# Two attentions with column-half value products, full-height score passes and single column sums: a change to block 2 of a two-block transformer kernel

## The chip, the core and the metric

The kernel runs on one core of one Trainium2 chip. The metric is the device time of one execution in microseconds (us), as a median of several runs. The core's engines are named as in the profile: PE multiplies matrices, PEld is the loading of its stationary operand, DVE, ACT and POOL are the vector, scalar and GpSimd engines, SP issues the transfers. A product on PE takes a stationary operand (rows of contraction by output rows) and streams a moving operand through it, column by column; the result lands in one of eight PSUM banks of 128 partitions by 512 fp32 columns. A row of the profile that says `128*64 128x512` is a stationary operand of 128 rows by 64 columns with 512 moving columns.

## What is computed

Two transformer blocks run over 512 tokens of width 1024, all in float32 precision. Only block 2's mixer matters in detail:

```python
u = rms_norm_2(h, mix_norm[i]);  proj = u @ w_in[i]
c_q, c_kv, k_rope, sb_qkv, gates = jnp.split(proj, SPLITS, axis=-1)
...
o_mla = causal_softmax_attention(q, k, v_mla)          # 8 heads, 96 wide, values 64 wide
o_sb = stick_breaking_attention(sq, sk, sv)            # 8 heads, 64 wide, values 64 wide
g_mla, g_sb = jnp.split(jax.nn.sigmoid(gates), 2, axis=-1)
merged = g_mla * (o_mla @ w_branch_mla[i]) + g_sb * (o_sb @ w_branch_sb[i])
h = h + merged @ w_out[i]
```

The stick-breaking weights are `exp(log_sigmoid(z) + suffix)`, where `suffix` sums `log_sigmoid(-z)` over the keys behind; they need no division. The softmax weights of the latent heads do. Each block also has feed-forward parts, and every norm divides by the root of a mean of squares over the 1024 features.

## The kernel before

Activations are kept feature-major (features on the 128 partitions, the 512 tokens along the free axis). A product in float32 is made of three passes over exact parts: high by high, low by high and high by low (`lin`, lines 259 to 261), or is one float32 matmul that PE runs as two passes. Weights stream in from HBM; ACT and DVE split each piece (lines 247 and 248).

`mixer2` (from line 880) is block 2's attention part. It is written as generators, one for each head and one for each chunk of a projection, and the string `STEPS2` says in which order their steps are issued: a digit is a step of stick-breaking head `sb(h)`, a letter a step of latent head `mla(h)`, `.` and `,` a step of the large projections, which fill PE's time while ACT and DVE work on a head. A scheduler then settles each engine's order from that.

A stick-breaking head has three steps. The first makes the scores `z` (lines 942 to 944): for each of four key blocks a pass of the stacked keys (high and low halves on 128 rows) against the queries, a bf16 pass that adds the mask (stationary operand: an identity), and a pass of the 64 rows of high keys against the queries' low part `ql`. The second makes the suffix sums. The third is the value product (line 984): the head's weights `za` stream past a 64-column piece of the values, and the result takes one half of a PSUM bank, the partitions 0 to 63 for even heads, 64 to 127 for odd ones. Two heads share the bank, and when both are in, ACT and DVE split it into exact parts (`split`, lines 310 and 311).

A latent head has five steps: transposes of queries and keys (line 1113), scores and softmax (lines 1128 to 1137; ACT adds up each row's sum), transposes of the weights (`et`, line 1144), the value product (line 1155), and, for each second head, four transposes (line 1169) and a split. In the value product the weights are stationary and 64 columns of values stream, token-major: 10 blocks of 128 by 128, two passes each. DVE then multiplies each token block by the reciprocal of its sum (line 1160). PSUM is shared out as two banks for projections, three for scores, two ("t") for transposes and one ("o") for the value products.

A norm's sum of squares (`Squares`) is kept as two tiles: ACT squares the chunks of features, POOL adds the first seven into `acc`, the last stays in its own tile. `colsum` (line 335) sums both over the partitions on PE with a moving operand of one column of ones: for each of four token blocks one matmul of `acc` and one of the last square, in two passes each.

## Time and profile before

| | us |
|---|---|
| median of 3 runs | 2273.33 (2273.32 to 2273.71) |
| span of the profiled execution | 2267.5 |
| own time of the profiled execution | not given; the runs lie 5.8 above the span |
| PE busy | 2247.1 (99%) |
| PEld, DVE, ACT, POOL busy | 1870.9, 1151.6, 881.5, 119.6 |

Busy times are shares of the span, not proof of a bound: a busy PE may be streaming, loading or draining. The stage that the change touches most lies between 1420 and 1840 us of the span. Most readings below go by when one instruction on PE starts and when the next does, since the printed length of a pass includes its overlap with the next.

### The profile page before, as it was taken

Reading aid. Unit: us, or ns where it says so; the run is one execution under the profiler, and the core shown is the slowest. Engines: PE = TensorE matmul, PEld = TensorE weight load, DVE = VectorE, ACT = ScalarE, POOL = GpSimd, SP = SyncE. Lnnn points to the kernel's source line nnn. Section 1 sums busy time; section 2 is a strip of 40 time slices with the busy share of each in tenths; the row PEclk is TensorE's granted clock in tenths of the full one; section 3 lists DMA queues with packets and bytes.
Section 4 is the critical chain, followed back from the end, with each engine's and each line's share of the span. In section 5 each row is a group of like instructions: output and inputs, shape, how many; then the busy total and the mean of one; then the engine's idle time right before and its main releaser. Section 6 shows DMA issues by size and latency. Waiting matters only on the chain.

```text
span 2267.5 us, 27653 instructions
## 1 busy us (share of the span) xinstructions
PE 2247.1 (99%) x11074; PEld 1870.9 (83%) x11074; DVE 1151.6 (51%) x1938; ACT 881.5 (39%) x1344; POOL 119.6 (5%) x156
## 2 busy tenths in 40 slices
PE   8999999999999999999999999999999999999999
PEld 7888888888788888889888888877778888888887
DVE  5644323778648444325644433476674654444334
ACT  4323223556635333223432322566654442233222
POOL 3000001000112000001000001000000010000000
PEclk9999999999889999999999999999999999999999
DMA  5333333322112333332333333321131233333331
GB/s 151 93 96 100 95 94 91 88 62 75 38 47 85 102 93 102 93 96 73 112 93 101 89 96 104 85 66 48 46 89 34 79 112 94 102 93 96 96 107 65
DMA packets 364836, 197.22 MB, mean 87 GB/s; under 512 B 10007, under 2 KB 356516, under 8 KB 364708
## 3 DMA queue, kind: packets, MB, share of 16 engines
q1 hardware_dynamic: 364100, 195.37, 30.0%
q8 instruction: 87, 1.43, 0.3%
q0 software_dynamic: 608, 0.09, 0.0%
q14 instruction: 41, 0.34, 0.0%
HBM read 193.33 MB, written 2.10 MB: 86 GB/s over the span
## 4 chain that ended last, share of the span: by engine, by line
PE 98%; DVE 1%; ACT 0%; DMA 0%; issue 0%; SPq 0%; DVEq 0%
PE f1o_p L260 2%; PE f2o_p L259 2%; PE f2o_p L260 2%; PE f1o_p L259 2%; PE f2o_p L261 2%; PE f1o_p L261 2%; PE f4o_p L259 2%; PE f3o_p L261 2%; PE f4o_p L261 2%; PE f3o_p L259 2%; PE f3o_p L260 2%; PE f4o_p L260 2%; PE gt_p L260 1%; PE gt_p L259 1%; PE gt_p L261 1%; PE f_p L260 1%
## 5 line engine op out<-in xcount | busy, mean ns | idle before, releaser
L248 DVE TENSOR_TENSOR f1o_l<-f1o_r,f1o_h 128x1024 fp32r<-128x1024 f32 (+1 forms) x24 | 27.3, 1136 | 76.6 <-ACT f1o_h L247 76.6
L248 DVE TENSOR_TENSOR f2o_l<-f2o_r,f2o_h 128x1024 fp32r<-128x1024 f32 (+1 forms) x24 | 27.3, 1136 | 76.6 <-ACT f2o_h L247 76.6
L247 ACT ACTIVATE f2o_h<-f2o_r 128x1024 fp32r<-128x1024 f32 (+1 forms) x24 | 23.8, 990 | 85.7 <-PE f2o_p L260 73.0
L247 ACT ACTIVATE f1o_h<-f1o_r 128x1024 fp32r<-128x1024 f32 (+1 forms) x24 | 23.8, 990 | 85.7 <-PE f1o_p L260 68.4
L247 ACT ACTIVATE f3o_h<-f3o_r 128x1024 fp32r<-128x1024 f32 (+1 forms) x24 | 23.8, 990 | 85.3 <-PE f3o_p L260 53.2
L247 ACT ACTIVATE f4o_h<-f4o_r 128x1024 fp32r<-128x1024 f32 (+1 forms) x24 | 23.8, 990 | 85.0 <-PE f4o_p L260 52.8
L376 POOL TENSOR_TENSOR f_acc<-f_acc,f_sq 128x256 f32<-128x256 f32 (+1 forms) x42 | 38.9, 927 | 316.9 <-ACT f_sq L375 299.5
L248 DVE TENSOR_TENSOR f3o_l<-f3o_r,f3o_h 128x1024 fp32r<-128x1024 f32 (+1 forms) x24 | 27.3, 1136 | 54.0 <-ACT f3o_h L247 54.0
L248 DVE TENSOR_TENSOR f4o_l<-f4o_r,f4o_h 128x1024 fp32r<-128x1024 f32 (+1 forms) x24 | 27.3, 1135 | 52.5 <-ACT f4o_h L247 52.5
L84 ACT ACT_TABLE_LOAD x36 | 46.2, 1283 | 1.4 <-PEq L1341 0.8
L376 POOL TENSOR_TENSOR m_acc<-m_acc,m_sq 128x256 f32<-128x256 f32 (+1 forms) x18 | 20.1, 1115 | 348.8 <-ACT m_sq L375 348.8
L260 PE MATMUL m1o_p<-mix_l,m1o_h 128*128 128x256 f32 (+1 forms) x88 | 29.3, 334 | 0.0
L261 PE MATMUL m1o_p<-mix_h,m1o_l 128*128 128x256 f32 (+1 forms) x88 | 29.2, 334 | 0.0
L259 PE MATMUL m1o_p<-mix_h,m1o_h 128*128 128x256 f32 (+1 forms) x88 | 28.6, 336 | 0.0
L376 POOL TENSOR_TENSOR pl_acc<-pl_acc,pl_sq 128x512 f32<-128x512 f32 x6 | 10.3, 1710 | 341.6 <-ACT pl_sq L375 341.6
L248 DVE TENSOR_TENSOR gt_l<-gt_r,gt_h 128x1024 fp32r<-128x1024 f32 x16 | 19.6, 1224 | 12.9 <-ACT gt_h L247 12.6
L94 ACT ACTIVATE l<-l 128x384 f32<-128x384 f32 (+1 forms) x48 | 24.2, 554 | 3.1 <-DVE l L949 3.0
L247 ACT ACTIVATE pg_h<-pg_r 128x1024 fp32r<-128x1024 f32 x8 | 8.5, 1061 | 42.6 <-PE pp L496 19.4
L94 ACT ACTIVATE e<-ms,mx,sck 128x512 f32<-128x512 f32 (+3 forms) x32 | 19.5, 614 | 14.0 <-DVE mx L1135 13.8
L260 PE MATMUL wo_p<-mg_l,wo_h 128*128 128x512 f32 x64 | 24.8, 390 | 0.0
L259 PE MATMUL wo_p<-mg_h,wo_h 128*128 128x512 f32 x64 | 24.8, 389 | 0.0
L376 POOL TENSOR_TENSOR f2p_acc<-f2p_acc,f2p_sq 128x512 f32<-128x512 f32 x6 | 7.7, 1288 | 322.9 <-ACT f2p_sq L375 322.9
(4287 smaller groups left out, 7533.5 us busy)
## 6 DMA issues: line engine op xcount, KB each, us to landing
f1o_r<-in_ffn_w_out_dram SPq DMA_DIRECT2D x16, 512.0 KB, 3.8
f2o_r<-in_ffn_w_out_dram SPq DMA_DIRECT2D x16, 512.0 KB, 4.3
f3o_r<-in_ffn_w_out_dram SPq DMA_DIRECT2D x16, 512.0 KB, 4.3
gt_r<-in_w_in_dram SPq DMA_DIRECT2D x16, 512.0 KB, 4.0
f4o_r<-in_ffn_w_out_dram SPq DMA_DIRECT2D x16, 512.0 KB, 4.1
f_r<-in_ffn_w_in_dram SPq DMA_DIRECT2D x12, 512.0 KB, 5.0
mg_r<-in_w_mix_in_dram SPq DMA_DIRECT2D x8, 512.0 KB, 4.0
m1o_r<-in_w_mix_out_dram SPq DMA_DIRECT2D x8, 512.0 KB, 4.2
```

What stands on the lines that cost most here:

```text
L84: ld = S.preload_act_table_set(name).ins
L94: i = S.activation(out, in_, func, **kw).ins
L247: S.activation(hi, raw, AF.Copy)
L248: V.tensor_tensor(lo, raw, hi.bitcast(F32), ALU.subtract)
L259: M.matmul(o, w[0], u[0], start=first, stop=False)
L260: M.matmul(o, w[0], u[1], start=False, stop=False)
L261: issued["last"] = M.matmul(o, w[1], u[0], start=False, stop=last).ins.name
L376: G.tensor_tensor(acc[:, sl], acc[:, sl], q[:, sl], ALU.add)
```

## The change

**Scores.** The low part of the queries is held in two tiles of 128 rows, one for each head, with zeros in the half that is not the head's own. POOL writes the zeros (eight of them, 64 by 512). The third pass of each piece is then 128 rows high, uses the same stationary keys as the first, and comes before the mask's pass.

**Value products.** `av_pair` issues the products of two heads in turn, key block by key block, one head into the lower and one into the upper half of one bank. It is called once both heads' weights are there, so the stick-breaking heads use four visits of PE, not eight. The latent heads now use the same form: the values are stationary (64 columns) and the transposed weights stream. The `et` transposes are as many as before, grouped by key block.

**Normalisation of the latent heads.** The result is feature-major at once, so the four transposes of the output go. The reciprocals of two heads (one DVE instruction) are widened by POOL to 128 by 512 (`rcw`), transposed by four PE instructions (`rcs`), copied to SBUF by ACT, and one DVE multiplication of 128 by 512 takes the place of eight of 128 by 64; the split reads that product from SBUF.

**Column sums.** In seven norms (three in block 1, three in block 2, one in the last part) one DVE addition of 128 by 512 joins the two tiles of squares, and `colsum` gets one tile.

**Order.** `STEPS2` is written anew for four steps a latent head. The order of the transfers on SP does not change.

The core of the diff (comments and docstrings that went are left out):

```diff
-STEPS2 = ('00..110,.3,2,2..3.4,,4.56241.56,,7,..s3567q.7ka.ba,cbca,,,d,a.,ccbdebg,,bdc.e..,.e.,.a.f,d,hgffd'
-          ',,e,gh,,eh,,f,,.,g,gh,fh')
+STEPS2 = ('00..110,.3,2,2..3.4,,4.56241.56,,7,..s3567q.7kaab,,bc,a,cd,b,de,ca,ef,db,fg,ec,gh,fd,h,ge,hfg'
+          '')
@@ Normed.factor (and the same two lines in ple)
-            r = token_rs(self.sq.parts, D, self.name)
+            acc, q = self.sq.parts
+            V.tensor_tensor(acc, acc, q, ALU.add)
+            r = token_rs([acc], D, self.name)
@@ sb_qk
-                ql = A(f"sql{j}", F32R)
-                for t, own in ((s0, lo), (s1, up)):
+                ql = [A(f"sql{j}{i}", F32R) for i in range(2)]
+                for t, l, own, other in ((s0, ql[0], lo, up), (s1, ql[1], up, lo)):
+                    G.memset(l[other, :].bitcast(F32), 0.0)
...
-                    V.tensor_tensor(ql[own, :], a[own, :], t[own, :].bitcast(F32), ALU.subtract)
+                    V.tensor_tensor(l[own, :], a[own, :], t[own, :].bitcast(F32), ALU.subtract)
@@ sb
                 M.matmul(z, k[:, b], q[:, t0:], start=True, stop=False)
-                M.matmul(z[:, d:d + P], identb, nst, start=False, stop=False)
-                M.matmul(z, k[own, b], ql[own, t0:], start=False, stop=True)
+                M.matmul(z, k[:, b], ql[:, t0:], start=False, stop=False)
+                M.matmul(z[:, d:d + P], identb, nst, start=False, stop=True)
...
-            other = pair.pop(h ^ 1, None)
-            o = pair[h] = px(f"osb{h}") if other is None else other
-            for c, l in enumerate(parts(za)):
-                M.matmul(o[own, c * P:], sv[c][:, h * 64:(h + 1) * 64], l, start=c == 0, stop=c == NT - 1)
-            if other is not None:
+            pair[h] = parts(za)
+            if h ^ 1 in pair:
+                o = px(f"osb{h}")
+                av_pair(o, lambda c, g: sv[c][:, g * 64:(g + 1) * 64], pair, h & ~1)
                 osb[h // 2] = split(o, f"osb{h}")
             yield
+        def av_pair(o, v, ps_, g):
+            for c in range(NT):
+                for i in (g, g + 1):
+                    M.matmul(o[64 * (i - g):64 * (i - g) + 64, c * P:], v(c, i), ps_[i][c], start=c == 0,
+                             stop=c == NT - 1)
@@ mla
-            ets = {}
-            for i, ts in enumerate(((3,), (2, 0), (1,))):
+            ets = [None] * NT
+            for i, ss in enumerate(((0,), (1, 3), (2,))):
                 ot, et = px(f"et{h}{i}", "t"), A(f"eT{h}{i}")
                 c = 0
-                for t in ts:
-                    for s in range(t + 1):
+                for s in ss:
+                    ets[s] = et[:, c:c + T - s * P]
+                    for t in range(s, NT):
                         M.transpose(ot[:, c:c + P], es[t][1][:, s * P:(s + 1) * P], ident)
-                        ets[t, s] = et[:, c:c + P]
                         c += P
...
-            oo = px(f"omla{h}", "o")
-            for t in (3, 2, 0, 1):
-                for s in range(t + 1):
-                    M.matmul(oo[:, t * 64:(t + 1) * 64], ets[t, s], vt[s][:, h * 64:(h + 1) * 64],
-                             start=s == 0, stop=s == t)
-            rc = tiny.tile([P, NT], F32, tag="rc", name=f"rc{h}")
-            V.reciprocal(rc, sums)
-            for t in range(NT):
-                V.tensor_scalar(om[t][:, h * 64:(h + 1) * 64], oo[:, t * 64:(t + 1) * 64], rc[:, t:t + 1], None,
-                                ALU.mult)
-            yield
-            j = h // 2
-            if omla[j] is None:
-                omla[j] = ()
-            else:
-                o = px(f"omT{j}", "t")
+            mpair[h] = ets
+            if h ^ 1 in mpair:
+                j = h // 2
+                oo = px(f"omla{j}", "o")
+                av_pair(oo, lambda c, g: vt[c][:, g * 64:(g + 1) * 64], mpair, h & ~1)
+                rc = tiny.tile([P, NT, 2], F32, tag="rc", name=f"rc{h}")
+                V.reciprocal(rc, msum[j])
+                sp, rw = px(f"rcs{j}", "t"), A(f"rcw{j}")
+                G.tensor_copy(rw.rearrange("p (t h n) -> p (t h) n", h=2, n=64),
+                              rc.rearrange("p t (h o) -> p (t h) o", o=1).to_broadcast([P, 2 * NT, 64]))
                 for t in range(NT):
-                    M.transpose(o[:, t * P:(t + 1) * P], om[t][:, j * P:(j + 1) * P], ident)
-                omla[j] = split(o, f"omT{j}")
+                    M.transpose(sp[:, t * P:(t + 1) * P], rw[:, t * P:(t + 1) * P], ident)
+                rs = A(f"rcs{j}")
+                S.activation(rs, sp, AF.Copy)
+                V.tensor_tensor(rs, oo, rs, ALU.mult)
+                omla[j] = split(rs, f"omT{j}")
```

How the order of instructions moves is shown at three places of PE. In the rows, what stands left of the arrow is written, right of it come the moving and then the stationary operand (for transposes the identity first); the trailing numbers are buffers.

**The scores of stick-breaking head 0**, the first two of its four pieces (`z` are banks, `sqk` queries and keys, `sql` the low part, `nst` and `identb` the mask's operands). Before:

```order
L942 MATMUL z00_11152<-sqk00_10962,sqk40_11004 128x512
L943 LDWEIGHTS identb_95
L943 MATMUL z00_11152<-nst_97,identb_95 128x128
L944 MATMUL z00_11152<-sql0_10965,sqk40_11004 128x512
L942 MATMUL z20_11154<-sqk00_10962,sqk40_11004 128x256
L943 LDWEIGHTS identb_95
L943 MATMUL z20_11154<-nst_97,identb_95 128x128
L944 MATMUL z20_11154<-sql0_10965,sqk40_11004 128x256
```

After:

```order
L944 MATMUL z00_11140<-sqk00_10947,sqk40_10992 128x512
L945 MATMUL z00_11140<-sql00_10950,sqk40_10992 128x512
L946 LDWEIGHTS identb_95
L946 MATMUL z00_11140<-nst_97,identb_95 128x128
L944 MATMUL z20_11142<-sqk00_10947,sqk40_10992 128x256
L945 MATMUL z20_11142<-sql00_10950,sqk40_10992 128x256
L946 LDWEIGHTS identb_95
L946 MATMUL z20_11142<-nst_97,identb_95 128x128
```

The pass of the low part has moved ahead of the mask's, next to the pass with the same keys, and reads a tile of its head's own; the later two pieces and the other heads follow suit.

**The stick-breaking value products.** Before, heads 2 and 4, both in the lower half of their banks (`za` followed by block and head, `sv` the values):

```order
L984 MATMUL osb2_12060<-za02_11551,sv0_11135 64x512
L984 MATMUL osb2_12060<-za12_11552,sv1_11137 64x384
L984 MATMUL osb2_12060<-za22_11553,sv2_11139 64x256
L984 MATMUL osb2_12060<-za22_11553,sv3_11141 64x128
L984 MATMUL osb4_12065<-za04_11822,sv0_11135 64x512
L984 MATMUL osb4_12065<-za14_11823,sv1_11137 64x384
L984 MATMUL osb4_12065<-za24_11824,sv2_11139 64x256
L984 MATMUL osb4_12065<-za24_11824,sv3_11141 64x128
```

After, heads 2 and 3, the first in the lower, the second in the upper half of one bank:

```order
L994 MATMUL osb3_12436<-za02_11540,sv0_11123 64x512
L994 MATMUL osb3_12436<-za03_11471,sv0_11123 64x512
L994 MATMUL osb3_12436<-za12_11541,sv1_11125 64x384
L994 MATMUL osb3_12436<-za13_11472,sv1_11125 64x384
L994 MATMUL osb3_12436<-za22_11542,sv2_11127 64x256
L994 MATMUL osb3_12436<-za23_11473,sv2_11127 64x256
L994 MATMUL osb3_12436<-za22_11542,sv3_11129 64x128
L994 MATMUL osb3_12436<-za23_11473,sv3_11129 64x128
```

Head by head has become head beside head. Three of the four stick-breaking pairs stand like this; the pair of heads 4 and 5 is cut in two visits of four rows. Of the latent pairs the first is spread over four visits (1, 1, 3 and 3 rows) and the other three stand whole.

**The end of the latent heads**, where the branch products `br` begin. Before (`omT` is the transposed output of a pair of latent heads, `om` the output of a token block):

```order
L1169 MATMUL omT2_14128<-ident_79,om3_13065 128x128
L261 MATMUL br03_p_14247<-omT0_h_13667,br03_0_l_14244 128x512
L259 MATMUL br03_p_14247<-omT1_h_13868,br03_0_h_14243 128x512
L260 MATMUL br03_p_14247<-omT1_l_13869,br03_0_h_14243 128x512
L261 MATMUL br03_p_14247<-omT1_h_13868,br03_0_l_14244 128x512
L1169 MATMUL omT3_14137<-ident_79,om0_13062 128x128
L1169 MATMUL omT3_14137<-ident_79,om1_13063 128x128
L1169 MATMUL omT3_14137<-ident_79,om2_13064 128x128
L1169 MATMUL omT3_14137<-ident_79,om3_13065 128x128
L259 MATMUL br00_p_14172<-omT2_h_14133,br00_0_h_14168 128x512
L259 MATMUL br01_p_14197<-omT2_h_14133,br01_0_h_14193 128x512
L259 MATMUL br02_p_14222<-omT2_h_14133,br02_0_h_14218 128x512
```

After (`rcs` are the transposed reciprocals, `eT` the weights, `vt` the values), with the end of pair 2's transposes and pair 3's value product:

```order
L261 MATMUL br03_p_14164<-omT1_h_13842,br03_0_l_14161 128x512
L1171 MATMUL rcs2_14024<-ident_79,rcw2_14025 128x128 x4
L994 MATMUL omla3_14038<-eT60_13943,vt0_12867 64x512
L994 MATMUL omla3_14038<-eT70_13995,vt0_12867 64x512
L994 MATMUL omla3_14038<-eT61_13950,vt1_12874 64x384
L994 MATMUL omla3_14038<-eT71_14002,vt1_12874 64x384
L994 MATMUL omla3_14038<-eT62_13957,vt2_12908 64x256
L994 MATMUL omla3_14038<-eT72_14009,vt2_12908 64x256
L994 MATMUL omla3_14038<-eT61_13950,vt3_12915 64x128
L994 MATMUL omla3_14038<-eT71_14002,vt3_12915 64x128
L259 MATMUL br00_p_14089<-omT2_h_14034,br00_0_h_14085 128x512
L259 MATMUL br01_p_14114<-omT2_h_14034,br01_0_h_14110 128x512
```

and a little later, the end of pair 3:

```order
L261 MATMUL br02_p_14139<-omT2_h_14034,br02_0_l_14136 128x512
L260 MATMUL br03_p_14164<-omT2_l_14035,br03_0_h_14160 128x512
L261 MATMUL br03_p_14164<-omT2_h_14034,br03_0_l_14161 128x512
L1171 MATMUL rcs3_14049<-ident_79,rcw3_14050 128x128 x4
L259 MATMUL br00_p_14089<-omT3_h_14059,br00_0_h_14085 128x512
L259 MATMUL br01_p_14114<-omT3_h_14059,br01_0_h_14110 128x512
```

Before, products of other tiles stood between the transposes and the first product that needs their result. Now `omla3`, which needs the one "o" bank, stands right behind `rcs2`, and the first product of `omT3_h` right behind `rcs3`. For pairs 0 and 1 eight transposes (of `qkT` and of `et`) stand between `rcs` and the next pair's value product.

## Rows read from the trace of the kernel before

**Rows 1.** The page, part 4: the chain that ended last, by engine.
```profile
PE 98%; DVE 1%; ACT 0%; DMA 0%; issue 0%; SPq 0%; DVEq 0%
```

**Rows 2.** Busy time by stretch of mixer2; stretch, length, busy times, PEclk, DMA, GB/s.
```profile
1460.00:1540.00 80.00, 80.00 (x354) 62.05 (x353) 59.41 (x97) 54.90 (x99) 0.00 (x0) 1.00 0.26 66
...
1620.00:1660.00 40.00, 40.00 (x201) 32.27 (x201) 33.93 (x138) 24.43 (x55) 0.00 (x0) 1.00 0.24 66
...
1420.00:1840.00 420.00, 420.00 (x2050) 333.43 (x2048) 260.29 (x571) 230.31 (x429) 11.66 (x7) 1.00 0.26 69
```

**Rows 3.** Timeline of PE, one head's scores; start, length (us), then the instruction.
```profile
1560.47 0.40 PE L260 MATMUL cq_p<-m_u6l,cq_h 128*128 128x512 f32 x1
1560.71 0.40 PE L942 MATMUL z<-sqk,sqk 128*128 128x512 f32 x1
1560.95 0.23 PE L943 MATMUL z<-nst,identb 128*128 128x128 bf16 x1
1561.11 0.50 PE L944 MATMUL z<-sql,sqk 64*128 64x512 f32 x1
1561.54 0.39 PE L942 MATMUL z<-sqk,sqk 128*128 128x256 f32 x1
...
1563.75 0.50 PE L261 MATMUL cq_p<-m_u6h,cq_l 128*128 128x512 f32 x1
```

**Rows 4.** Timeline of PE, a mask's pass of a latent head and its successor.
```profile
1699.53 0.22 PE L1129 MATMUL ms<-nts,identb 128*128 128x128 bf16 x1
1699.59 0.86 PE L1128 MATMUL ms<-qkT,qkT 96*128 96x384 f32 x2
```

**Rows 5.** Timeline of PE, value products: one head; two heads in the same half.
```profile
1542.74 0.39 PE L261 MATMUL gt_p<-m_u7h,gt_l 128*128 128x512 f32 x1
1543.06 2.37 PE L984 MATMUL osb<-za,sv 128*64 128x512 f32 x8
1545.36 0.50 PE L259 MATMUL cq_p<-m_u0h,cq_h 128*128 128x512 f32 x1
...
1565.78 4.52 PE L984 MATMUL osb<-za,sv 128*64 128x512 f32 x16
1570.23 0.50 PE L260 MATMUL gt_p<-m_u1l,gt_h 128*128 128x512 f32 x1
```

**Rows 6.** Timeline of PE, head 5's last two passes (upper half), head 6's eight (lower).
```profile
1608.96 2.38 PE L984 MATMUL osb<-za,sv 128*64 128x128 f32 x10
1611.27 0.38 PE L335 MATMUL cq_ss<-ones,cq_last 128*128 128x1 f32 x2
```

**Rows 7.** Timeline of PE, block 1: 512 columns in one, two and four column groups.
```profile
441.68 0.68 PE L663 MATMUL pd<-X 128*64 128x64 f32 x8
442.95 0.45 PE L663 MATMUL pd<-X 128*32 128x32 f32 x16
449.00 0.39 PE L663 MATMUL pd<-X 128*16 128x16 f32 x32
```

**Rows 8.** Timeline of PE, the last latent head's value product and what follows.
```profile
1775.88 2.34 PE L1155 MATMUL omla<-vt,eT 128*128 128x64 f32 x20
1778.05 0.61 PE L1169 MATMUL omT<-ident,om 128*128 128x128 f32 x4
1778.42 0.49 PE L261 MATMUL br_p<-omT_h,br_l 128*128 128x512 f32 x1
```

**Rows 9.** Timeline of PE, sixteen passes of a norm's column sum, first, last, successor.
```profile
2218.79 0.28 PE L335 MATMUL pl_ss<-ones,pl_acc 128*128 128x1 f32 x2
...
2220.27 0.36 PE L335 MATMUL pl_ss<-ones,pl_last 128*128 128x1 f32 x2
2220.50 0.48 PE L495 MATMUL pg<-pg_h,pl_u6h 128*128 128x512 f32 x1
```

**Rows 10.** Timelines of ACT and DVE behind the transposes of rows 8.
```profile
1778.70 0.60 ACT L310 ACTIVATE omT_h<-omT 128x512 fp32r<-128x512 f32 x1 [4.09 <-PE omT L1169]
...
1779.33 0.69 DVE L311 TENSOR_TENSOR omT_l<-omT,omT_h 128x512 fp32r<-128x512 f32 x1 [0.21 <-ACT omT_h L310]
```

**Rows 11.** Groups of POOL and of DVE: line, operation, count; busy, mean ns; idle.
```profile
L783 POOL COPY ws<-wd 128x128 f32<-128x128 f32 x4 | 1.2, 290 | 147.7 <-DVE wd L779 147.7
...
L1247 DVE TENSOR_TENSOR gate<-gate,gate 128x512 f32<-128x512 f32 x8 | 5.5, 688 | 0.0
```

**Rows 12.** Busy time of two stretches of block 1 with a stall; columns as in rows 2.
```profile
385.00:395.00 10.00, 8.82 (x61) 8.55 (x60) 9.90 (x25) 6.51 (x16) 3.09 (x5) 0.83 0.43 119
...
687.00:691.00 4.00, 2.93 (x23) 2.81 (x24) 3.85 (x9) 3.68 (x9) 0.59 (x1) 1.00 0.58 170
```

More of the change, by code (lines that the diff above doesn't have):

```diff
@@ L883, in mixer2 @@
         us, R, r = nx.factor()
-        sqk, sv, osb, pair, gate = {}, [], [None] * 4, {}, {}
+        sqk, sv, osb, pair, mpair, gate = {}, [], [None] * 4, {}, {}, {}
         bc = lambda a, n: a.rearrange("p (t o) -> p t o", o=1).to_broadcast([P, NT, n])
@@ L929, in sb @@
         def sb(h):
-            own = slice(64 * (h % 2), 64 * (h % 2) + 64)
-            q, k, ql = sqk[h // 2][h % 2], sqk[4 + h // 2][h % 2], sqk[h // 2][2]
+            q, k, ql = sqk[h // 2][h % 2], sqk[4 + h // 2][h % 2], sqk[h // 2][2][h % 2]
             width = (4 * P, 3 * P, 3 * P)
@@ L1076, in mixer2 @@
         sc, tk = (tiny.tile([P, NT, 8], F32, tag=f"sck{i}", name=f"sck{i}", bufs=1) for i in range(2))
-        qT, kT, om, omla = {}, {}, [], [None] * 4
+        qT, kT, msum, omla = {}, {}, {}, [None] * 4
         def head_factor(i, tl):
@@ L1117, in mla @@
             yield
-            if not om:
-                om.extend(A(f"om{t}") for t in range(NT))
-            sums = tiny.tile([P, NT], F32, tag="sums", name=f"sums{h}")
+            if h % 2 == 0:
+                msum[h // 2] = tiny.tile([P, NT, 2], F32, tag="sums", name=f"sums{h}")
+            sums = msum[h // 2][:, :, h % 2]
             es = [None] * NT
@@ L1287, in ple @@
                     pT.append(split(o, f"pT{j}"))
-                rs.append(token_rs(nx.sq.parts, D, "pl", behind=issued["last"]))
+                acc, q = nx.sq.parts
+                V.tensor_tensor(acc, acc, q, ALU.add)
+                rs.append(token_rs([acc], D, "pl", behind=issued["last"]))
                 table("sigmoid_and_others")
```

## The prediction

> **What bounds the kernel now.** I read the chain of waits first: PE has 98% of it [rows 1]. Then the busy time by stretch, for the stage that the change touches: between 1420 and 1840 us PE is busy in 420.00 of 420.00 us at a granted clock of 1.00 (2.4 GHz), DVE in 260.29, ACT in 230.31 and POOL in 11.66 [rows 2]. DVE comes nearest in the stretch from 1620, 33.93 of 40 us. So whatever PE no longer issues in this stage comes off the end, as long as nothing makes PE wait; and every new wait of PE is paid in full. How much a piece of PE work costs is not its printed length but the distance from its start to the start of what follows, so all prices below are differences of starts in the timeline of PE.
>
> **Scores.** One head's twelve passes run from 1560.71 to 1563.75 [rows 3]: 3.04 us. In them a 128-row pass of 512 columns takes 0.24 (1560.71 to 1560.95), the mask's pass 0.16, and the 64-row pass of 512 columns 0.43 (1561.11 to 1561.54): it is slow, and the mask ahead of it too, while a latent head's mask, followed by a pass of 96 rows, takes 0.06 [rows 4]. After the change a head has two 128-row passes for 1408 columns, 2816 in all at 0.24 for 512: 1.32 us. The masks lie between 4 x 0.06 and 4 x 0.16; no row shows a mask between two full-height passes, so I take 0.11, 0.44 in all. That is 1.76 a head, 1.28 saved, times eight **10.2 us** (8.6 with the dear mask, 11.8 with the cheap one). The zeros for the low part cost eight instructions on POOL, which is idle there [rows 2], and are written before the subtraction that fills the other half; I price them at nothing. Were they late, the first score pass of a pair would wait about as long as a POOL instruction of that size takes; the nearest row, a copy of 128 by 128, takes 0.29 [rows 11].
>
> **Stick-breaking value products.** One head's eight passes take 2.30 us from start to next start, two heads in the same half 4.45 [rows 5]. So halves of the array that stand idle are not given back when two heads share one half. Whether two different halves overlap is told by one visit that the scheduler made by chance: two passes of 128 columns of head 5 (upper half) and all eight of head 6 (lower half) take 2.31 [rows 6], as long as head 6 alone would. The two upper passes cost nothing. Block 1 says the same within a single PSUM bank: 512 columns in one column group take 0.68, in two alternating groups 0.45, in four 0.39 [rows 7]. So I price a pair at one head's 2.30. A visit has an edge: the pass ahead of the solo head takes 0.32 (1542.74 to 1543.06) where 0.23 is usual, and the one behind it lasts 0.50 for 0.39 [rows 5]; together 0.2. Before: eight heads at 4.45 a couple, 17.8, and seven visits' edges, 1.4: 19.2. After: four pairs, 9.2, and five edges: 10.2. Saved: **9.0 us**.
>
> **Latent value products.** Before, the last head's twenty passes of 64 columns take 2.17 (1775.88 to 1778.05) [rows 8], eight heads 17.4. After, three whole pairs at 2.5 with the edge are 7.5. The first pair is spread over four visits, partly alone: 512 columns, 512, 640 and 384, against 1280 of a whole head, so 1.6 times 2.30, 3.7, and four edges, 0.8: 4.5. Saved: 17.4 - 12.0 = **5.4 us**. The four transposes of a pair are replaced by four. The thirty-two small multiplications on DVE go, four of 128 by 512 come; DVE is not the bound, so neither counts by itself.
>
> The Trainium skill ("TensorEngine Tiling (Array Packing)", Key Properties) says that a change of tiling mode drains the TensorE, which speaks against the new visits of the latent heads, since those were in no column mode before. The trace agrees, at 0.2 us for both edges [rows 5], which is in the sum.
>
> **Column sums.** Sixteen passes take 2218.79 to 2220.50, 1.71 us [rows 9]; half of them go, 0.855, in seven norms **6.0 us**. The added DVE addition takes 0.69 [rows 11] and stands ahead of the sum; in every one of the seven norms PE has other products between the last square and the column sum, so I price it at nothing. Where that cover is missing it costs at most 0.69 of the 0.855: 4.8 us over all seven, which is the lower bound (1.2).
>
> The four gains make 10.2 + 9.0 + 5.4 + 6.0 = 30.6 us.
>
> **The new waits.** After `rcs` comes a chain that the old kernel did not have: ACT copies the bank, DVE multiplies out of the "o" bank, ACT splits. In the old tail the first product behind the transposes starts at 1778.42 [rows 8], ACT's copy at 1778.70 for 0.60, DVE's at 1779.33 for 0.69 [rows 10]. So the "o" bank is free 1.60 us after PE could have gone on, and another 0.60 of ACT and 0.03 of hand-over later, at 2.23, the high part is there. What PE has to do meanwhile is told by the order. `omla3` stands right behind `rcs2`: 1.60 lost. The first product of `omT3_h` stands right behind `rcs3`: 2.23. Behind `rcs0` and `rcs1` come eight transposes, 0.37 for four [rows 8], so 1.60 - 0.74 = 0.86 each. Sum: **5.5 us**. Before the `rcs` transposes POOL widens the reciprocals, about 4 x 0.29 = 1.2 us by its copy [rows 11]; it needs only the softmax sums, which are complete before the `et` transposes start, so I price it at nothing. On SP nothing moves.
>
> The net is 30.6 - 5.5 = 25.1 us. The profiled execution's own time is not given; its span is 2267.5 and the runs' median lies 5.8 above. I take these off the median: 2273.3 - 25.1 = **2248.2**, and say 2248.
>
> **Rivals.**
>
> *Passes start in program order.* A head's two passes of one matmul must follow one another, so if starts keep to program order the upper head's first pass begins with the lower head's second. Each pair is then longer by one pass of 512 columns, nearly: 2.30 holds 2560 columns, so 512 are 0.46; seven whole pairs give 3.2 us: 2251. In the visit of ten passes that order would have put the lower half's start behind the first upper pass, at least 0.1 later than measured [rows 6]. The Trainium skill ("TensorE: Matmul & The Clock Gate", Part 3) states that matmuls start and end strictly in program order; by that rule this case would be the likely one, and the visit of ten passes does not bear it out. Chance 0.12.
>
> *The halves do not overlap for long passes.* The visit of ten passes has only 128 columns beside 512. If two long streams share a limit, a pair takes 4.45: the stick-breaking heads gain only two edges, 0.4, and the latent ones lose 4 x 4.65 - 17.4 = 1.2 and three more edges for the scattered pair, 0.6. Then 10.2 + 0.4 - 1.8 + 6.0 - 5.5 = 9.3: 2264. Against it: four column groups in block 1 run faster than one [rows 7]. Chance 0.06.
>
> *The waits are longer.* All four pairs pay the whole 2.23 and the 1.2 of POOL, 13.7 in place of 5.5: 2256. Besides, PE may fall to 1.2 GHz behind a stall: from 385 to 395 us, a stretch with 1.18 us of idle PE, the mean granted clock was 0.83 [rows 12], 3.4 us at the low level and 1.7 lost; from 687 to 691, with 1.07 idle, it stayed at 1.00 [rows 12]. Two such falls give 2260. For it speaks that the chains cross three engines and that ACT also splits weights in this stage; against it that ACT and DVE idle in over a third of it [rows 2]. Chance 0.14.
>
> *Slower: each alternation drains the array.* If going from one half to the other stops the array until the pass before has left it, then every one of some 64 alternations of the eight pairs has a price, and the halves do not overlap either. Take the mask ahead of a 64-row pass as that price: 0.16 for 0.06, 0.10 more [rows 3, 4]. Then 64 x 0.10 = 6.4 on top of the case above leaves 2.9 of gain: 2270. The point of no gain is a price of 0.145 (9.3 / 64); above 0.215 the kernel is slower by over 0.2%, and at 0.30 it takes 2283. The passes of block 1 that alternate between two groups come faster than those that stay in one [rows 7], which all but excludes it. Chance 0.04, half of it above 0.215.
>
> **How the numbers follow.** The forecast has the remaining 0.64: 2248, its own bounds 2243 (cheap mask, waits half hidden, no edges: 1.6, 2.7 and 1.0) and 2254 (dear mask, additions of squares half exposed, one fall of the clock: 1.6, 2.4, 1.7). The range from 2240 to 2260 takes in the rivals of program order and of longer waits, and leaves out the two at the top. A measurement of this kernel can tell about 0.2%, 4.5 us, from no change. The first three rivals and the forecast are all faster by more than that, 0.96; I take 0.01 off for waits several times those priced. Faster 0.95; within 0.03, which is that 0.01 and half of the last rival; slower 0.02, its other half.
>
> **What would show it.** In the timeline of PE after, a head's scores should take about 1.76 from start to next start, a visit of sixteen value passes 2.3 to 2.5 (2.8 by program order, 4.5 without overlap), a column sum of eight passes 0.86. The idle time of PE should grow by about 5.5 us, in four places, each ending with DVE's multiplication or ACT's split. I am wrong if PE waits in the stick-breaking part, where it has no idle time now, if the visits of sixteen passes take over 3 us, or if the granted clock falls below 1.00 between 1420 and 1800 us.

## The result, and the profile after

The changed kernel took 2244.74 us (median of 4 runs, 2241.62 to 2247.31) against 2273.52 (4 runs, 2273.32 to 2273.94): ratio 0.9881, 95% interval 0.9859 to 0.9903. A second set on another occasion gave 2249.25 (6 runs) against 2271.27 (12 runs), ratio 0.9898 (0.9878 to 0.9917). So it is about 1.1% faster, 22 to 29 us; 25 were forecast.

That the two sets differ by almost 7 us goes with something that the runs list: the mean clock granted to TensorE. Over the 161 timed runs that list it, it lay between 0.988 and 0.996 (between 0.989 and 0.996 for the kernel before alone), and each 0.001 less went with 1.70 us more (a straight line with one constant for each kernel, and one more for the second set; what it leaves over is 1.0 us a run). In the traces most of the low stretches lie in block 1, between 600 and 640 us. Below, "at equal clock" means the difference of these constants: the changed kernel is 22.2 ± 1.1 us faster in the first set, 21.6 ± 0.9 in the second. The four runs of the kernel before in the first set list no clock, so the constant of the kernel before comes from its 62 other runs. Each listed run lies some 1.8 us above its own span; of the 5.8 by which the first runs lay above the profiled span, the rest is then a difference of executions.

Still less noisy is the stage from the first projection of block 2's mixer to the last product of the feed-forward part behind it, where the clock is 1.00 but for one fall shown below. Its windows in the kernel before and in the changed one (stretch, length, busy times of PE, PEld, DVE, ACT, POOL, PEclk, DMA, GB/s):

```profile
1421.52:2200.96 779.44, 779.44 (x3644) 631.40 (x3643) 411.56 (x749) 338.03 (x559) 21.91 (x13) 1.00 0.29 81
```

```profile
1417.20:2178.67 761.47, 756.28 (x3533) 610.95 (x3531) 409.15 (x719) 338.54 (x563) 26.45 (x21) 1.00 0.30 83
```

18.0 us shorter, with 111 instructions of PE fewer, and with 5.19 us in which PE is idle, where it never was idle before. The chain shows the same change: ACT has come into it, where it had 0% [rows 1].

```profile
PE 97%; DVE 1%; ACT 1%; DMA 0%; issue 0%; SPq 0%; DVEq 0%; ACTq 0%
```

One head's scores and, right behind them, one pair's value products, in PE's timeline of the changed kernel:

```profile
1541.09 0.39 PE L944 MATMUL z<-sqk,sqk 128*128 128x512 f32 x1
1541.31 0.39 PE L945 MATMUL z<-sql,sqk 128*128 128x512 f32 x1
1541.54 0.23 PE L946 MATMUL z<-nst,identb 128*128 128x128 bf16 x1
1541.58 0.36 PE L944 MATMUL z<-sqk,sqk 128*128 128x256 f32 x1
1541.78 0.28 PE L945 MATMUL z<-sql,sqk 128*128 128x256 f32 x1
...
1542.90 2.37 PE L994 MATMUL osb<-za,sv 128*64 128x512 f32 x16
1545.21 0.50 PE L260 MATMUL cq_p<-m_u5l,cq_h 128*128 128x512 f32 x1
```

The pass of the low part takes 0.23 (1541.31 to 1541.54) where the 64-row pass took 0.43 [rows 3]. The mask takes 0.04, and the pass behind it 0.20 where the other pass of 256 columns takes 0.12: a mask costs 0.12 with what it adds to its successor, and 0.11 was taken. The head takes 1.81 instead of 3.04. Sixteen value passes of two heads take 2.31, what one head's eight took [rows 5]. A narrower cut of the timeline, the first 50 ns of this visit, shows why:

```profile
1542.90 0.65 PE L994 MATMUL osb<-za,sv 128*64 128x512 f32 x2
```

Two passes have begun, one in each half (7 ns apart in the trace), and the second passes of both begin 0.48 later, as one head's would alone.

The end of the latent heads on PE, and what ACT and DVE do there:

```profile
1749.76 0.60 PE L1171 MATMUL rcs<-ident,rcw 128*128 128x128 f32 x4
1751.77 2.37 PE L994 MATMUL omla<-eT,vt 128*64 128x512 f32 x16 [1.41 <-DVE rcs L1174]
1754.08 1.19 PE L259 MATMUL br_p<-omT_h,br_h 128*128 128x512 f32 x4
...
1756.94 0.60 PE L1171 MATMUL rcs<-ident,rcw 128*128 128x128 f32 x4
1759.61 2.07 PE L259 MATMUL br_p<-omT_h,br_h 128*128 128x512 f32 x4 [2.07 <-ACT omT_h L310]
```

```profile
1757.58 0.60 ACT L1173 ACTIVATE rcs<-rcs 128x512 f32<-128x512 f32 x1 [5.20 <-PE rcs L1171]
1758.93 0.63 ACT L310 ACTIVATE omT_h<-rcs 128x512 fp32r<-128x512 f32 x1 [0.76 <-DVE rcs L1174]
```

```profile
1758.21 0.69 DVE L1174 TENSOR_TENSOR rcs<-omla,rcs 128x512 f32<-128x512 f32 x1 [5.10 <-ACT rcs L1173]
```

The chain runs as it was drawn from rows 10: transposes, ACT 0.60, DVE 0.69, ACT 0.63, and PE has nothing else. Behind `rcs0` and `rcs1`, where eight other transposes stand, the value product comes 2.02 and 2.01 us after the start of `rcs`, nearly as late as behind `rcs2` (1749.76 to 1751.77, 2.01):

```profile
1701.00 0.60 PE L1171 MATMUL rcs<-ident,rcw 128*128 128x128 f32 x4
...
1703.02 0.65 PE L994 MATMUL omla<-eT,vt 128*64 128x512 f32 x2
...
1733.04 0.60 PE L1171 MATMUL rcs<-ident,rcw 128*128 128x128 f32 x4
...
1735.05 0.65 PE L994 MATMUL omla<-eT,vt 128*64 128x512 f32 x2
```

The window around the last wait shows that the clock fell as well:

```profile
1750.00:1765.00 15.00, 11.52 (x53) 8.18 (x52) 5.17 (x8) 4.27 (x7) 0.00 (x0) 0.89 0.00 0
```

0.11 of 15 us is 1.7 us lost, 3.4 us at 1.2 GHz; the trace has the lower clock from 1759.5 us on, while the wait ended at 1759.61. And the stick-breaking part waits too, which had no idle time:

```profile
1560.49 0.45 PE L973 MATMUL y<-lx2h,ntrir 128*128 128x384 f32 x1 [0.30 <-ACT lx2h L959]
...
1564.32 0.38 PE L978 MATMUL y<-s,nonesr 128*128 128x256 f32 x1 [0.19 <-ACT s L959]
1564.87 0.35 PE L335 MATMUL cq_ss<-ones,cq_acc 128*128 128x1 f32 x2 [0.16 <-DVE za L980]
```

### The profile page after: what moved, and what is told of

Read it like the earlier page. It is cut to its first block, busy times and chain, and to the rows that moved or that the text cites. A ratio compares the mean times of both kernels' runs of the same rounds, so it can differ in the third digit from the quotient of the medians.

```text
span 2244.3 us, 27350 instructions
## 1 busy us (share of the span) xinstructions
PE 2218.9 (99%) x10922; PEld 1844.9 (82%) x10922; DVE 1151.8 (51%) x1913; ACT 881.6 (39%) x1348; POOL 126.3 (6%) x168
## 4 chain that ended last, share of the span: by engine, by line
PE 97%; DVE 1%; ACT 1%; DMA 0%; issue 0%; SPq 0%; DVEq 0%; ACTq 0%
PE f1o_p L259 2%; PE f2o_p L260 2%; PE f1o_p L260 2%; PE f2o_p L259 2%; PE f2o_p L261 2%; PE f1o_p L261 2%; PE f4o_p L260 2%; PE f4o_p L259 2%; PE f3o_p L259 2%; PE f3o_p L260 2%; PE f3o_p L261 2%; PE f4o_p L261 2%; PE gt_p L259 1%; PE gt_p L260 1%; PE gt_p L261 1%; PE f_p L260 1%
## 5 line engine op out<-in xcount | busy, mean ns | idle before, releaser
L376 POOL TENSOR_TENSOR f1p_acc<-f1p_acc,f1p_sq 128x512 f32<-128x512 f32 x6 | 7.7, 1288 | 321.5 <-ACT f1p_sq L375 321.5
L261 PE MATMUL wo_p<-mg_h,wo_l 128*128 128x512 f32 x64 | 24.7, 389 | 0.0
L247 ACT ACTIVATE pg_h<-pg_r 128x1024 fp32r<-128x1024 f32 x8 | 8.5, 1061 | 39.9 <-PE pg L498 12.7
```

The lines of the kernel that those rows point to most:

```text
L247: S.activation(hi, raw, AF.Copy)
L261: issued["last"] = M.matmul(o, w[1], u[0], start=False, stop=last).ins.name
L376: G.tensor_tensor(acc[:, sl], acc[:, sl], q[:, sl], ALU.add)
```

## The experiments

### Each part alone

Four kernels hold one part of the change each; the edits are the corresponding pieces of the diff above, the rest is the kernel before. The window of the stage follows each.

*Scores alone* (`sb_qk` and the z loop of `sb`).

> The kernel before with the change of the score passes alone (low part of the queries in two zero-filled tiles of 128 rows, mask last). The sum of the prediction gives 10.2 us for it: 2273.5 - 10.2 = 2263.3. In the trace of the changed kernel the starts of the 96 score passes are 13.33 us apart in all, against 22.81 before, so 9.5: 2264.0. Rival (the scores are cheaper but the heads' chains through ACT and DVE do not follow, and PE waits in the stick-breaking part as it does at 1559.85 us of the changed kernel, 0.30 + 0.19 + 0.16): the gain is under 8 and PE shows new idle time before 1640 us.

Measured: 2261.06 against 2271.26, ratio 0.9951 (0.9934 to 0.9968), 11.4 ± 0.7 faster at equal clock.

```profile
1422.14:2190.18 768.04, 768.04 (x3645) 627.25 (x3643) 410.49 (x749) 337.51 (x559) 24.63 (x17) 1.00 0.29 82
```

779.44 - 768.04 = 11.4, and PE is never idle: the rival falls, and the term was 1.2 too small. From start to next start the 96 score passes give 9.65 of it (22.81 to 13.16), the passes of the suffix sums 1.08 (17.60 to 16.52), the value products 0.43 (18.17 to 17.74). POOL's eight writes of zeros are in it and cost nothing.

*Stick-breaking pairs alone* (`av_pair` and the third step of `sb`).

> The kernel before with the value products of the stick-breaking heads alone issued by av_pair. If halves overlap, 64 passes take about 9.4 us from start to start instead of 18.2 and with their edges 10.4 instead of 19.9: 9.0 to 9.4 us off, 2264.3. If they overlapped only beside short passes: a visit of sixteen takes 4.5 and the gain is under 1 us. If passes start in program order one by one: 2.8 a visit and 6 us of gain, 2267.5.

Measured: 2265.21, ratio 0.9972 (0.9958 to 0.9986), 8.1 ± 0.6 at equal clock.

```profile
1419.57:2190.55 770.98, 770.06 (x3644) 627.95 (x3643) 411.89 (x749) 337.44 (x559) 22.59 (x13) 1.00 0.29 82
```

8.5 us, with 0.92 of new idle time: PE waits in two places (0.30 for ACT, 0.62 for DVE). The halves overlap in full. That the waits come because a visit of a single head no longer stands between the suffix sums is read from the order and was not tested.

*Column sums alone* (`factor` and `ple`).

> The kernel before with the two tiles of squares added by DVE ahead of the column sum, in the seven norms. Forecast: eight passes go in each, 7 x 0.855 = 6.0, and the additions are hidden: 2267.5. Rival: the additions (0.69 each) are in PE's way and 0.17 a norm is left, 1.2 in all: 2272.3; then PE would wait for DVE ahead of the column sums.

Measured: 2262.66, ratio 0.9964 (0.9952 to 0.9977), 5.1 ± 0.7 at equal clock; the mean clock of its runs was 0.9938, so the raw difference is 8.6. In the traces m2 and f4 together take 1.53 off the stage (779.44 to 777.91) and pl 0.89 (19.42 to 18.53 from the last product of the part ahead to the last pass of the sum). The sixteen passes of f1 took 1.70, the eight take 0.81. In the stage PE is never idle (777.91 of 777.91 us), so the rival, that PE waits for the additions, falls there.

In m1, f2 and f3 the old kernel sums the tokens in two halves, eight passes for the first half long before the rest, and there little or nothing is saved where the clock is 1.00. The measure is again from the last product of the part ahead to the last pass of the sum, and only traces at the same clock may be compared: in many of them 3.4 us at the low level fall into m1 or f3. First m1, then f3, each with sixteen passes at either clock and then with eight. The kernels are, line by line, *stick-breaking pairs alone*, before, *column sums alone* and changed for m1; before, the five sums, the two early pairs (both further down) and *column sums alone* for f3. The columns are those of the windows above, with PE alone.

```profile
384.28:412.66 28.38, 27.20 (x221) 1.00 0.17 45
384.86:413.85 28.99, 27.81 (x221) 0.94 0.16 43
383.62:411.84 28.22, 27.04 (x212) 1.00 0.17 43
383.33:411.53 28.20, 27.02 (x213) 0.94 0.17 45
```

```profile
1054.99:1083.37 28.38, 27.20 (x220) 1.00 0.15 42
1048.61:1077.86 29.25, 28.07 (x221) 0.94 0.15 42
1056.04:1084.61 28.57, 27.24 (x212) 1.00 0.15 42
1051.65:1080.22 28.57, 27.33 (x212) 0.94 0.14 42
```

At 1.00 the change saves 0.16 in m1 and loses 0.2 in f3; f2, always at 1.00, goes from 28.43 to 28.27. With the low stretch it saves 0.8 in m1 and 0.7 in f3 (0.2 by the trace of *stick-breaking pairs alone*, 28.79). With eight passes the clock makes no difference: there PE has time to spare, as its products go at the pace of the chunks that DVE makes (in f3 of the kernel before DVE works without a pause from 1073.91 to 1079.95 us). In f3 they arrive at the last eight passes no earlier when the first eight are gone (27.68 us before, 27.87 in both traces with eight). Sixteen passes used that time up, and then the low clock cost 0.6 to 0.9 in all traces but one (0.4). So at full clock what was saved there had been free. Why f3 loses 0.2 is open.

*Latent heads alone* (`mla`, `av_pair` and the new `STEPS2`).

> The kernel before with the change of the latent heads alone (values stationary, pairs of heads, normalisation feature-major, new order of the steps). Theory: in the changed kernel the value products take 10.9 us for 16.9 before, 5.9 off; against it 5.2 us of idle PE, and transposes that are dearer by 2.8 (et 1.15, qkT 0.98, rcs 0.64 over omT), mostly the array running empty ahead of a wait; so this part alone is worth -2, within 2 us of 2275.5. Rival (the sum of the prediction): 5.4 - 5.5, nothing: 2273.5. Rival (the waits of the changed kernel come from its shorter score and value passes and do not show here): 4 to 6 us off, 2268.5.

Measured: 2274.77, ratio 1.0018 (1.0005 to 1.0031), slower by 0.6 ± 0.6 at equal clock.

```profile
1422.26:2204.18 781.92, 777.61 (x3548) 619.67 (x3547) 407.26 (x717) 340.05 (x563) 24.83 (x17) 1.00 0.29 81
```

2.48 longer, 1.7 of it the fall of the clock at the last wait. All the waits of the changed kernel's latent heads are there (4.31 us idle; the last is 1.84). So this part is no gain: the value products save 5.9 (16.85 to 10.93 from start to next start), and that is given back, as the forecast had it (5.4 - 5.5), and a little more.

*The four parts together.* The parts alone add up to 11.4 + 8.1 + 5.1 - 0.6 = 24.0 ± 1.3 at equal clock. For the second set of the changed kernel 23.6 had been expected by that sum, and the two sets gave 22.2 and 21.6, about two less.

### What makes two heads run side by side

```diff
-            for c in range(NT):
-                for i in (g, g + 1):
+            for i in (g, g + 1):
+                for c in range(NT):
                     M.matmul(o[64 * (i - g):64 * (i - g) + 64, c * P:], ...
```

> The changed kernel with the two loops of av_pair swapped: all four matmuls of the lower head are issued, then the four of the upper head. Theory A (matmuls begin in the order of issue, and only a neighbour in the other half can run beside one): only the lower head's last matmul, 128 columns, meets the upper head's first; a visit of sixteen passes takes 4.45 - 0.2 = 4.2 to 4.4 instead of 2.30, seven whole pairs cost 13 to 15 more: 2258 to 2260. Theory B (each half has a queue of its own and PE looks far ahead): a visit stays at 2.3 and the time within 2 us of the changed kernel.

Measured: 2261.83 against 2271.27, 12.7 slower than the changed kernel at equal clock. A visit:

```profile
1545.96 3.93 PE L994 MATMUL osb<-za,sv 128*64 128x512 f32 x16
1549.82 0.50 PE L260 MATMUL cq_p<-m_u5l,cq_h 128*128 128x512 f32 x1
```

3.86 us, as in each of the six whole visits. That is between the theories, so neither stands as put, though the time is nearly that of theory A. In the trace of this visit the upper head's first pass starts at 1547.522, with the first pass of the lower head's third matmul (1547.517), and ahead of three passes that were issued before it (1547.732, 1547.948 and 1548.057). PE does start a product for the free half out of turn, but here only over the last two matmuls ahead of it: it did not start beside the first or the second one. That is why the alternation is needed. The Trainium skill ("TensorE: Matmul & The Clock Gate", Part 3) says that matmuls start and end strictly in program order. Here it is not so: besides these starts, in the alternating kernel the second passes of one matmul start behind the first pass of the next.

### Without the latent part

The kernel before, with three of the four parts; against the changed kernel:

```diff
-STEPS2 = ('00..110,.3,2,2..3.4,,4.56241.56,,7,..s3567q.7kaab,,bc,a,cd,b,de,ca,ef,db,fg,ec,gh,fd,h,ge,hfg'
+STEPS2 = ('00..110,.3,2,2..3.4,,4.56241.56,,7,..s3567q.7ka.ba,cbca,,,d,a.,ccbdebg,,bdc.e..,.e.,.a.f,d,hgffd'
+          ',,e,gh,,eh,,f,,.,g,gh,fh')
...
-                av_pair(oo, lambda c, g: vt[c][:, g * 64:(g + 1) * 64], mpair, h & ~1)
+            for t in (3, 2, 0, 1):
+                for s in range(t + 1):
+                    M.matmul(oo[:, t * 64:(t + 1) * 64], ets[t, s], vt[s][:, h * 64:(h + 1) * 64],
+                             start=s == 0, stop=s == t)
...
```

> The kernel before with the scores, the stick-breaking pairs and the column sums changed, and the latent heads with their order of steps as before. The parts alone measured 11.3 + 8.0 + 4.9 at equal granted clock, so 24.2 faster than before and 0 to 2 us faster than the changed kernel; the waits behind the rcs transposes are gone and the 160 short value passes are back. Rival (the latent part pays only together with the others, because they shorten what stands between its waits): 2 us or more slower than the changed kernel.

Measured: 2244.79 (4 runs), ratio 0.9883 (0.9863 to 0.9903), 22.0 ± 1.1 at equal clock, the changed kernel's gain.

```profile
1415.52:2174.28 758.76, 758.10 (x3629) 622.62 (x3628) 412.41 (x751) 337.18 (x559) 24.66 (x17) 1.00 0.30 83
```

The stage is 2.7 us shorter than with the latent part; 1.7 of that is the fall of the clock. The three parts alone make 11.4 + 8.5 + 1.5 = 21.4 here, together 20.7. Of the 0.7 between them, 0.43 were counted twice: the scores alone had shortened the value products by that much, and with the pairs these take 9.37 with or without the scores' change. The rival, that the latent part pays together with the others, falls.

### The reciprocals' chain ahead of the value product

```diff
+            if h ^ 1 in mready:
+                rc = tiny.tile([P, NT, 2], F32, tag="rc", name=f"rc{h}")
+                V.reciprocal(rc, msum[h // 2])
+                rw = A(f"rcw{h // 2}")
+                G.tensor_copy(rw.rearrange("p (t h n) -> p (t h) n", h=2, n=64),
+                              rc.rearrange("p t (h o) -> p (t h) o", o=1).to_broadcast([P, 2 * NT, 64]))
             ets = [None] * NT
...
+            if h ^ 1 in mready:
+                sp = px(f"rcs{h // 2}", "t")
+                for t in range(NT):
+                    mlast[h // 2] = M.transpose(sp[:, t * P:(t + 1) * P], rw[:, t * P:(t + 1) * P], ident).ins.name
+                rs = A(f"rcs{h // 2}")
+                S.activation(rs, sp, AF.Copy)
+            mready.add(h)
             yield
             mpair[h] = ets
...
-                av_pair(oo, lambda c, g: vt[c][:, g * 64:(g + 1) * 64], mpair, h & ~1)
+                av_pair(oo, lambda c, g: vt[c][:, g * 64:(g + 1) * 64], mpair, h & ~1, mlast[j])
...
-                S.activation(rs, sp, AF.Copy)
```

`av_pair`'s matmuls are also kept in turn behind the transposes. The second kernel does this for the last two pairs alone.

> The changed kernel with the reciprocals, their widening on POOL, the four rcs transposes and ACT's copy moved into the step of the et transposes of a pair's second head, ahead of the value product, and the eight matmuls of a pair kept in turn behind them. What is left behind the value product is one DVE multiplication (0.69) and one split. If the chain behind rcs makes the waits, the idle time of PE in the latent heads falls from 4.5 us to under 1.5 and the kernel is 3 to 5 us faster than the changed one at equal granted clock. Rival (the one bank o makes them, whatever stands ahead of it): the wait moves to DVE's multiplication behind the value product and 2 us or less are won.

> The changed kernel with the reciprocals' chain (DVE, POOL, four rcs transposes, ACT's copy) ahead of the value product for the last two latent pairs alone, and every pair's matmuls kept in turn. In the changed kernel these two pairs hold the long waits, 1.41 and 2.07, and the second is followed by 3.4 us at the low clock. If that is what the chain costs: idle PE in the latent heads falls to about 1.5, the stretch at the low clock near 1756 us goes, and from the first product of the projections to the last of f4 the kernel takes 3 to 5 us less than the changed one's 761.5. Rival (as with all four pairs early, the reciprocal stands in DVE's queue ahead of other heads' work): new waits of 1 us or more ahead of et transposes, and less than 2 us won.

Measured: with all four pairs 2244.07, 22.5 ± 0.9 at equal clock; with the last two 2242.84 (5 runs) against 2272.56, ratio 0.9872 (0.9853 to 0.9891), 25.8 ± 0.9 at equal clock, 4 us better than the changed kernel. The stage of the first, then of the second:

```profile
1416.14:2175.43 759.29, 755.87 (x3533) 610.37 (x3531) 408.66 (x719) 338.94 (x563) 27.00 (x21) 1.00 0.29 83
```

```profile
1422.62:2178.64 756.02, 754.30 (x3533) 609.97 (x3532) 408.52 (x719) 338.10 (x563) 26.43 (x21) 1.00 0.30 84
```

With all four the expectation was missed: 3 to 5 us had been expected, and at equal clock the kernel is within 1 us of the changed one; idle time in the latent heads falls to 2.8, not under 1.5. The two long waits go, as put, but a new one comes, in another place than the rival said:

```profile
1687.78 1.23 PE L1159 MATMUL et<-ident,e 128*128 128x128 f32 x8 [1.54 <-ACT qkT L1123]
```

ACT is late there. Its last exponential (1686.49) waits for a maximum that DVE makes at 1686.31, behind the multiplication of the first pair (from 1685.70, 0.69 long). This is read from the trace; a kernel with that multiplication elsewhere was not run.

With two, idle time falls from 5.19 to 1.72, nothing replaces it, the clock stays up, and the stage is 5.45 us shorter than the changed kernel's: more than the 3 to 5 expected. The value product of the last pair now follows its transposes without a wait, and the products of the pair before stand behind it, while DVE and ACT finish:

```profile
1755.51 0.60 PE L1168 MATMUL rcs<-ident,rcw 128*128 128x128 f32 x4
1756.04 2.38 PE L994 MATMUL omla<-eT,vt 128*64 128x512 f32 x16
1758.35 1.20 PE L259 MATMUL br_p<-omT_h,br_h 128*128 128x512 f32 x4
```

So the chain behind `rcs` made the two long waits, and another place for it was enough, with the one "o" bank as it was. Whether a second bank would have done as well was not tried.

### Column sums, and the clock

Two kernels take the change of the sums apart: f1 and m1 alone on the kernel before, and all but f2 and f3 on the kernel without the latent part (there the names are f1, m1, m2 and f4, and pl is changed too).

```diff
-            acc, q = self.sq.parts
-            V.tensor_tensor(acc, acc, q, ALU.add)
-            r = token_rs([acc], D, self.name)
+            parts = self.sq.parts
+            if self.name in ("f1", "m1"):
+                V.tensor_tensor(parts[0], parts[0], parts[1], ALU.add)
+                parts = parts[:1]
+            r = token_rs(parts, D, self.name)
```

> The kernel before with the single column sum in two norms of block 1 alone (f1, ahead of the first feed-forward part, and m1, ahead of its mixer). From the traces with and without the change these two norms are worth about 0.8 us each: 1.6 off at equal granted clock. The mean granted clock was 0.9934 over 38 runs with all column sums changed and 0.9916 over 79 without (0.001 is 1.7 us between runs of one kernel). Theory: what shifts it lies at or ahead of the low stretch in block 1's mixer, so this kernel too runs at 0.993 or more and its median is 4 to 5 us below that of before. Rival: the sums of the other norms or chance; then its mean clock is that of before and the median 1.6 lower.

> The kernel before with scores and stick-breaking pairs changed, the latent heads as before, and the column sums changed in five norms (f1, m1, m2, f4, pl), not in f2 and f3. In f2 and f3 the traces show nothing saved (from the last product of the part before to the last pass of the sum 28.43 before and 28.28 after, 28.38 and 28.57). So the time at equal granted clock is that of the kernel without the latent part, 22 to 24 below before, within 0.5. Rival (all seven norms give their 0.86): 1.7 slower than that.

Measured: f1 and m1 alone 2265.99 against 2272.56, ratio 0.9983 (0.997 to 0.9996), 1.75 ± 0.64 at equal clock, as worked out. Its mean clock was 0.9931, with a standard error of 0.0007, beside 0.9916 (0.0005) in the runs of the kernel before beside it: in line with the first theory, but twelve runs do not exclude the rival. The five sums 2242.40, ratio 0.9884 (0.9865 to 0.9902), 22.3 ± 0.9 at equal clock beside 22.0 ± 1.1 with seven: no difference that these runs can tell, as expected. But the 28.38 and 28.57 from which this was expected, and the 0.8 for m1, compare stretches at different clocks. With the low stretch in both, f3 takes 29.25 with the old sums and 28.57 with the new, so the old sums are not free in every run.

Both findings together:

> The kernel of tail_early with the column sums of f2 and f3 as before. If both findings hold it is the fastest of this study: 0 to 0.5 us from tail_early at equal granted clock, and 24 to 26 below before there.

Measured: 2242.54 (4 runs), ratio 0.9877 (0.9857 to 0.9897), 25.0 ± 1.1 at equal clock, 0.9 behind the early chain for two pairs with all seven sums, which these runs cannot tell from nothing. Either of the two is 2.5 to 4 us ahead of the other kernels at equal clock, and they are the best of the study.

## Why the prediction was right, point by point

**Forecast 2248, range 2240 to 2260; measured 2244.74.** PE bounds the stage and what it no longer issues came off: right. That the number came so near is in part luck. The forecast took off 25.1; at equal clock the gain is 22, three less, and the rest of the 28.8 is, by the line above, the clock. Of the terms, the scores' came out too small and all others too large, which partly cancels. By terms, beside the trace of each part alone:

- *Scores*, 10.2, measured 11.4. One head of the changed kernel takes 1.81 for the 1.76 forecast. But the head that was read before (3.04) stands by itself: over all eight heads the score passes took 2.85 a head before and 1.65 after, 9.65 in all. The term was too small because it looked at score passes alone. The passes of the suffix sums gave 1.08 more; six of them had stood right behind a 64-row pass, where 384 columns took 0.28 for 0.17 now. The value products gave 0.43.
- *Stick-breaking pairs*, 9.0, measured 8.5. A visit takes 2.31 for 2.30; 0.92 of waits was not foreseen. The step that was wrong is that nothing in the stick-breaking part would wait, for which the prediction named the sign; in the changed kernel the waits there are 0.65.
- *Latent value products and waits*, 5.4 - 5.5, measured -0.8 without the clock. The value products gave 5.9. The four waits behind `rcs` were sized well: 2.02, 2.01, 2.01 and 2.67 us from the start of `rcs` to the instruction that waits are, less 0.37 for four transposes and 0.74 for the eight behind the first two, 0.91, 0.90, 1.64 and 2.30, where 0.86, 0.86, 1.60 and 2.23 had been taken. Not foreseen were 0.46 of waiting ahead of the first `qkT` behind the branch products, for ACT, and shorter delays at other transposes; whether those are the array running empty ahead of a wait, as was put for the latent heads alone, no run shows. So the idle time is in eleven places, not in four, though its sum is 5.19 for 5.5.
- *Column sums*, 6.0, measured 3.4 in the traces at clock 1.00 (0.9 in f1 by its passes, 1.5 in m2 and f4, 0.9 in pl, 0.1 in m1, f2 and f3 together), up to 4.9 where the low clock falls into m1 and f3, and 5.1 ± 0.7 between runs. The step that failed is that half the passes go in every one of the seven norms: in m1, f2 and f3 they had stood where PE goes at the pace of DVE's chunks and had cost next to nothing at full clock. What hides an added instruction had been considered; that the same cover could hide the passes removed had not.
- *The clock*: one fall of 3.4 us at a long wait, 1.7 us, was in the range and not in the sum; a clock below 1.00 in this stage was also named as a sign of being wrong. It came in each of the four traces that hold the last wait (1.84 to 2.08 idle), and in none without it.

These make 11.4 + 8.5 - 0.8 and 3.4 to 4.9 for the sums, less the 0.7 by which the parts overlap: 21.8 to 23.3 at equal clock, where 21.6 and 22.2 were measured. The raw 28.8 of the first set is larger, by the line above, for the clock of block 1, which no row of one trace could give.

**Rivals.** Program order (2.8 a visit) and halves without overlap (4.5) fell with the visits of 2.31; drained alternations too. Longer waits came true in one fall of the clock and 0.2 us, inside the range.

## What to carry over

Two products with 64 output rows each cost as much as one when they are issued in turn into the two column halves; issued one head behind the other they overlap only at the seam (3.86 us for 2.31). Before a normalisation is moved behind such a product, look at what stands behind its last transpose in the order: a chain over three engines with nothing to fill it took back the whole gain here, and moving what does not depend on the product ahead of it got most of it back, where nothing else in the queues of DVE and ACT was put off by it (two pairs, not four). When passes are removed, ask of each place whether PE was short of work there already, and compare two traces of it only at the same granted clock.

## What had not been expected of the hardware

The mean granted clock differs from run to run by up to 0.007, 12 us, for one and the same kernel. It was 0.9935 over the 65 runs of kernels with the column sums of block 1 changed and 0.9916 over the 96 without (standard errors 0.0002 each), and 0.9931 in the 12 runs where f1 and m1 alone were changed. Why shorter column sums should move the low stretches near 620 us was not found out; it may be no more than the instant at which that part of the program starts. Part of the gain of the medians, about 3 us, hangs on it.
